# HGRN2's two pairs, SSD and LRU as lanes of their own, LRU in the buffers of the normed tokens, and four lanes for RWKV's scan

## The chip, the cores and the metric

The kernel runs on one core of a Trainium2 chip. The metric is the device time of one execution, in microseconds (us). TensorE (PE in the profile) does the matmuls and transposes, VectorE (DVE) and ScalarE (ACT) the elementwise work, GpSimd (POOL) a little of it, and SyncE (SP) issues the loads and stores.

## The reference

One inference step of a trunk with two layers on 384 tokens (128 of context, 256 latent) of width 1024, in float32. In each layer the normed and modulated tokens are projected to four head groups of width 256, each scanned forward and backward; their outputs are concatenated and projected back. Then follows an MLP of hidden width 4096.

```python
def trunk_layer(x, mod, lw, lb, shift_fn, states):
    h = rms_norm(x, lw['g_pre1']) * (1 + sc1) + sh1
    proj = h @ lw['w_in']
    p_rw, p_hg, p_ss, p_lr = jnp.split(proj, ...)
    y_rw, f_rw = rwkv7_mix(p_rw, lw, shift_fn, s_rw)   # 4 heads, state 64 x 64
    y_hg, f_hg = hgrn2_mix(p_hg, lw, lb, s_hg)         # 4 heads, gated linear attention
    y_ss, f_ss = ssd_mix(p_ss, lw, s_ss)               # short convolution, softplus dt, state 64 x 128
    y_lr, f_lr = rglru_mix(p_lr, lw, s_lr)             # short convolution, gates, a diagonal scan, gelu
    mix = jnp.concatenate([y_rw, y_hg, y_ss, y_lr], axis=-1) @ lw['w_out']
    x = x + g1 * rms_norm(mix, lw['g_post1'])
    h = rms_norm(x, lw['g_pre2']) * (1 + sc2) + sh2
    ff = jnp.square(jax.nn.relu(h @ lw['w1'])) @ lw['w2']
    return x + g2 * rms_norm(ff, lw['g_post2']), (f_rw, f_hg, f_ss, f_lr)
```

LRU, for one direction: `a = exp(log_a)`, `b = sqrt(1 - a*a) * (i * xc)`, the scan `h = a*h + b`, and at the end `(h_fw + h_bw) * gelu(y)`. The final context states of all four groups are outputs too.

## The kernel before

A layer is a mixer (`mixers`), then an MLP (`mlp`). The mixer projects the 384 tokens into 29 tiles of 128 columns. A tile is 24 matmuls of 384 columns, since weights and tokens are each split into a high and a low part of a faster matmul type (`split_tile`: ScalarE copies the high part, L612, VectorE subtracts the low one, L613). `ORDER` is the order of the tiles: 0, 1, 3, 5 for RWKV, then nine of HGRN2 (7 to 16), then 2, 4, 6, then the rest of HGRN2, SSD (17 to 24) and LRU (25 to 28). Finished tiles stand in seven `st` buffers; a tile is projected only when the one seven places before it has been taken.

The scans are generators, called lanes. Before, there are five: three threads `t0` to `t2` that share twelve groups of RWKV's scan, `rwkv` (inputs, vectors and outputs of RWKV), and `right`, which runs HGRN2's first pair of heads, its second pair, SSD and LRU one after the other. Their programs work in rounds. In a round every lane is visited once and goes on to its next `yield`; a lane that yields a condition (`need(n)`: tile n has been projected) is passed over until it holds. Then `supply` issues projections, four matmuls (PSTEP) at a step, until the round holds 3000 ns by the kernel's own reckoning of TensorE's work in `Tensor.put` (ROUND), and a step of the later modulations every 1 / MODS rounds. If `right` waits, the projections of the round are made up to URGENT // PSTEP = 6 steps, one tile. TensorE's instructions are tied to this order by dependencies (`T.ordered`); the other engines' instructions are ordered by the framework. All matmuls go through one helper line, L239, so the trace's rows are told apart by tiles.

When `right` has ended, `tail` becomes a lane: the output projection in eight units of 128 rows (order HGRN2, SSD, LRU, then RWKV's first and second half), each for three token tiles of six matmuls with 512 columns; it fills the rounds in which RWKV's last groups run. After its last unit come post-norm, residual and the norm ahead of the MLP (`residual`).

Results in PSUM stand in a ring of banks, r0, r1, r2 and two of h (and md in layer 1); a lane's step takes the next one. Projections have two banks of their own (pj).

HGRN2's pair takes five tiles, then six levels of products within chunks, its state and its output. Its tiles stand in a pool on the right side of SBUF that is opened and closed for each of HGRN2, SSD and LRU in turn. The modulation's weights have a pool of their own (`mw`, three buffers). `ahead` is a pool with two `wh` and two `wl` buffers for the first weights of the next stage. The normed tokens stand split in `hhi` and `hlo`. LRU does all its elementwise work after the gates in one step, L805 to L843.

## Time and profile before

| | |
|---|---|
| median of 3 runs | 1448.69 us (1448.4 to 1454.03) |
| the profiled execution | 1454.01 us, its span 1452.2 us |
| busy, share of the span | TensorE 90%, VectorE 63%, ScalarE 39%, GpSimd 4% |
| mean granted TensorE clock | 0.949 |

The profile is of one execution. Busy time of TensorE is taken from modelled ends of pipelined matmuls. "x<-y" is the tile that an instruction writes and those that it reads, "<-" behind an idle time what ended it. L239 and L242 are matmul and transpose for all callers. An fp32 matmul appears as two instructions.

### The profile page before, as it was taken

The numbers are of one execution on the slowest core, as the hardware profiler recorded it, in microseconds if no ns is written. First come the engines' busy times: TensorE is split into PE (matmuls) and PEld (weight loads), VectorE is DVE, ScalarE is ACT, GpSimd is POOL, SyncE is SP. The second block draws the span as 40 slices with busy tenths as digits, with TensorE's granted clock in tenths as the row PEclk, the third lists the DMA queues.
The fourth block names the chain that finished last, engine by engine and source line by source line (L and its number), as shares of the span: only waits on it lengthen the run. The fifth ranks groups of instructions, "written<-read, shape, count | busy, mean of one in ns | idle before, by whom it ended". The sixth has DMA issues, their size and how long they took to land.

```text
span 1452.2 us, 29173 instructions
## 1 busy us (share of the span) xinstructions
PE 1306.4 (90%) x12128; PEld 1128.8 (78%) x12128; DVE 918.6 (63%) x2149; ACT 570.0 (39%) x1016; POOL 51.1 (4%) x100
## 2 busy tenths in 40 slices
PE   7899987996878989999989999978878789999997
PEld 2678976886556888899869898867766589889986
DVE  4576576868557878386364866776767676434534
ACT  4452323441634333244254533342345434324422
POOL 0001020000001000000000111000000000000000
PEclk9799998999978999999999999989989889999999
DMA  9544421110047866463452112110103453433333
GB/s 333 173 165 147 154 75 53 60 53 31 19 174 276 309 219 220 153 233 128 155 182 84 59 60 76 43 57 31 52 16 119 162 177 132 154 128 129 131 130 117
DMA packets 56321, 187.59 MB, mean 129 GB/s; under 512 B 6492, under 2 KB 9580, under 8 KB 55164
## 3 DMA queue, kind: packets, MB, share of 16 engines
q1 hardware_dynamic: 56188, 185.73, 37.2%
q8 instruction: 95, 1.56, 0.4%
q14 instruction: 38, 0.31, 0.1%
HBM read 178.28 MB, written 7.43 MB: 128 GB/s over the span
## 4 chain that ended last, share of the span: by engine, by line
PE 71%; DVE 18%; DMA 5%; ACT 4%; issue 2%; SPq 0%; POOL 0%; DVEq 0%; ACTq 0%; POOLq 0%
PE pj L239 33%; PE r L239 18%; PE h L239 13%; PE md L239 6%; DMA w<-in_mod_w_dram 2%; DVE wl L613 2%; DVE ma L491 2%; DMA ms<-in_mod_w_dram 1%; DMA gp<-in_norm_g_dram 1%; ACT wh L612 1%; DVE rP L1385 1%; ACT junk L534 1%; DVE x L603 1%; PE r L242 1%; DVE sx L781 1%
## 5 line engine op out<-in xcount | busy, mean ns | idle before, releaser
L613 DVE TENSOR_TENSOR wl<-raw,wh 128x1024 fp32r<-128x1024 f32 x202 | 247.3, 1224 | 252.3 <-ACT wh L612 249.8
L239 PE MATMUL pj<-hhi,wl 128*128 128x384 f32 (+2 forms) x1024 | 347.0, 339 | 7.9 <-DVE wl L613 7.8
L612 ACT ACTIVATE wh<-raw 128x1024 fp32r<-128x1024 f32 x202 | 214.0, 1059 | 357.1 <-PE md L239 151.9
L239 PE MATMUL pj<-hlo,wh 128*128 128x384 f32 (+2 forms) x1024 | 347.4, 339 | 4.7 <-DVE hlo L566 4.2
L239 PE MATMUL pj<-hhi,wh 128*128 128x384 f32 (+2 forms) x1024 | 349.2, 341 | 1.5 <-ACT relu L625 1.4
L239 PEld LDWEIGHTS pj<-hhi,wh 128*128 128x128 f32 x1024 | 197.8, 193 | 16.0 <-issue 7.6
L239 PEld LDWEIGHTS pj<-hhi,wl 128*128 128x128 f32 x1024 | 197.7, 193 | 11.5 <-DVE wl L613 9.2
L239 PEld LDWEIGHTS pj<-hlo,wh 128*128 128x128 f32 x1024 | 198.0, 193 | 10.4 <-DVE hlo L566 4.6
L491 DVE SCALAR_TENSOR_TENSOR ma<-ms,csil,ma 128x1024 f32<-128x1024 f32 x70 | 87.1, 1277 | 3.5 <-DMA ms<-in_mod_w_dram 3.5
L1412 DVE TENSOR_TENSOR rI<-rI,r 128x256 f32<-128x256 f32 (+1 forms) x69 | 26.5, 392 | 23.2 <-PE r L239 22.5
L239 PE MATMUL r<-rI,rW 64*64 64x64 f32 x552 | 35.0, 225 | 2.1 <-ACT li L802 1.3
L626 DVE TENSOR_TENSOR relu<-relu 128x384 f32<-128x384 f32 x64 | 35.3, 551 | 2.4 <-ACT relu L625 2.3
L625 ACT ACTIVATE relu<-pj 128x384 f32<-128x384 f32 x64 | 30.3, 474 | 13.1 <-PE pj L239 13.1
L239 PEld LDWEIGHTS r<-rI,rW 64*64 64x64 f32 x552 | 26.7, 136 | 9.4 <-issue 3.7
L239 PE MATMUL pj<-w,csil 128*32 128x512 f32 x64 | 22.3, 756 | 11.9 <-DMA w<-in_mod_w_dram 11.9
L239 PE MATMUL r<-rI,rP 64*64 64x64 f32 x512 | 25.8, 233 | 6.0 <-DVE rI L1394 4.3
L239 PEld LDWEIGHTS r<-rI,rP 64*64 64x64 f32 x512 | 20.5, 144 | 12.3 <-issue 4.1
L239 PE MATMUL r<-rW,rI 64*64 64x64 f32 x448 | 28.7, 221 | 0.0
L1401 DVE TENSOR_TENSOR rW<-r,cst 128x128 f32<-128x128 f32 x64 | 17.5, 286 | 14.5 <-PE r L239 14.0
L1112 ACT ACTIVATE hk<-hK 128x384 f32<-128x384 f32 x24 | 13.5, 563 | 32.3 <-PE h L239 11.3
L578 POOL TENSOR_TENSOR xs<-x,scale 128x512 f32<-128x512 f32 x9 | 13.0, 1443 | 373.6 <-ACT junk L534 248.0
L239 PE MATMUL h<-wh,o 128*128 128x512 f32 x64 | 24.3, 459 | 2.0 <-ACT o L1589 2.0
(909 smaller groups left out, 2583.3 us busy)
## 6 DMA issues: line engine op xcount, KB each, us to landing
raw<-in_w_dram SPq DMA_DIRECT2D x128, 512.0 KB
raw<-in_win_dram SPq DMA_DIRECT2D x58, 512.0 KB
mw<-in_mod_w_dram SPq DMA_DIRECT2D x40, 512.0 KB
ms<-in_mod_w_dram SPq DMA_DIRECT2D x40, 512.0 KB
w<-in_mod_w_dram SPq DMA_DIRECT2D x16, 512.0 KB
raw<-in_wout_dram SPq DMA_DIRECT2D x16, 512.0 KB
xd<-x SPq DMA_DIRECT2D x9, 512.0 KB
x<-xd SPq DMA_DIRECT2D x9, 512.0 KB
```

What stands on the lines that cost most here:

```text
L239: return self.put(self.engine.matmul(out, left, right, **k), left, right)
L242: return self.put(self.engine.transpose(out, left, right), left, right)
L491: V.scalar_tensor_tensor(acc[:, r, :], w, c, acc[:, r, :], op0=OP.mult, op1=OP.add)
L534: self.S.activation(junk, v, AF.Square, scale=1.0 / 32, accum_out=acc[:, i:i + 1])
L603: self.V.scalar_tensor_tensor(v, ys[n], r, v, op0=OP.mult, op1=OP.add)
L612: self.S.activation(hi, v, AF.Copy)
L613: self.V.tensor_sub(lo, v, hi.bitcast(F32))
L625: self.S.activation(r, ps[:, :NT], AF.Relu)
L626: self.V.tensor_mul(r, r, r)
L781: self.V.scalar_tensor_tensor(out, x[:, j:j + GAP], w[j], out, op0=OP.mult, op1=OP.add)
L1401: V.tensor_mul(w, ps[:, :128].rearrange("p (u s) -> p u s", u=2), self.c(f"w{'fb'[d]}{h}")[:, None, :].to_broadcast([128, 2, 64]))
L1412: V.tensor_sub(flat[:, f], flat[:, f], ps[:, 128 if h == 32 else 0:256].rearrange("p (q s) -> p q s", s=64))
```

## The change

HGRN2's two pairs become lanes `hg0` and `hg1`, each with its own tiles (`hgrn(l, p)`); what both share moves to `hgrn_start` and `hgrn_end`. `right` waits until both have ended, norms HGRN2's output, and goes on to SSD. LRU becomes a lane that waits for all 29 projections and for the modulations to be done; its `r`, `a` and `t` stand in the buffers of `hhi` and `hlo`, the rest in `ahead`, and its elementwise work is cut into rounds of their own. RWKV's scan gets a fourth thread. The modulation's weights stand in `ahead`'s `wh` buffers. `tail` begins when all four side lanes have ended. A whole tile is now issued in a round in which no side lane ran. ORD is 10: all ten tiles of HGRN2 stand ahead of tiles 2, 4 and 6. The unchanged body of HGRN2 is left out below.

```diff
-NSTASH, HELD, MW = 7, 3, 3
+NSTASH, HELD = 7, 3
...
-ORD = 9
+ORD = 10
...
-    def modulation(self, l, v, W, hold, pool, bufs=MW):
+    def modulation(self, l, v, W, hold, pool, bufs):
...
-                w.append(pool.tile([128, 1024], F32, tag="mw", name=self.name("mw"), bufs=bufs))
+                tag, dt = ("mw", F32) if pool is not self.ahead else ("wh", F32R)
+                w.append(pool.tile([128, 1024], dt, tag=tag, name=self.name("mw"), bufs=bufs).bitcast(F32))
...
     def lru(self, l):
+
         V, S, T = self.V, self.S, self.T
-        lrw = self.mt([128, 1024], "lrw")
+        yield lambda: len(self.turns) == NTILE and self.moded
+        unit = lambda t: self.ahead.tile([128, 1024], F32R, tag=t, name=self.name("lu"), bufs=FRESH).bitcast(F32)
+        pair = lambda z: z.rearrange("p (q t) -> p q t", q=2)
+        lrw, rest = unit("wl"), unit("wl")
         self.nc.sync.dma_start(lrw, self.a["lrw"][l])
-        s0 = self.state("s_lr", [2, 2])
-        xc = self.mt([128, 2, GAP], "lxc")
+        W = 2 * GAP
+        xc, nst, s0 = pair(rest[:, 0:W]), pair(rest[:, W:W + 4]), pair(rest[:, W + 4:W + 8])
+        self.nc.sync.dma_start(s0, self.a["s_lr"][:, l])
+        r, a, t, i = [], [], [], []
+        for z in self.split_buffers():
+            z = z.rearrange("p k t -> p (k t)").bitcast(F32)
+            for n, v in enumerate((r, a, t)):
+                v.append(pair(z[:, n * W:n * W + W]))
+            i.append(pair(unit("wh")[:, 0:W]))
...
-        r, i, a = (self.mt([128, 4, GAP], k) for k in ("lr", "li", "la"))
-        for g, dst, bias in ((0, r, "ba"), (1, i, "bx")):
+        for d in range(2):
+            for g, dst, bias in ((0, r[d], "ba"), (1, i[d], "bx")):
+                for hf in range(2):
+                    q = 2 * d + hf
+                    ps = self.bank()
+                    T.matmul(ps[:, :GAP], lrw[:, (g * 4 + q) * 128:(g * 4 + q + 1) * 128], xc[:, hf, :],
+                             start=True, stop=True)
+                    S.activation(dst[:, hf, :], ps[:, :GAP], AF.Sigmoid, bias=self.p(bias, q))
+                yield 1
+        for fn, dst in ((AF.Tanh, t), (AF.Exp, a)):
             for q in range(4):
...
         for d in range(2):
-            V.tensor_mul(i[:, 2 * d:2 * d + 2, :], i[:, 2 * d:2 * d + 2, :], xc)
-        V.tensor_mul(t, t, i)
+            V.tensor_mul(i[d], i[d], xc)
+        yield 1
+        for d in range(2):
+            S.activation(r[d], a[d], AF.Square)
+            V.scalar_tensor_tensor(t[d], r[d], 1.0, t[d], op0=OP.add, op1=OP.mult)
+            V.tensor_scalar(t[d], t[d], -1.0, 0.0, op0=OP.mult, op1=OP.max)
+        for d in range(2):
+            S.activation(t[d], t[d], AF.Sqrt)
+        yield 1
         h = r
-        nst = self.mt([128, 2, 2], "lst")
         for q in range(4):
             d, hf = divmod(q, 2)
+            if hf == 0:
+                V.tensor_mul(t[d], t[d], i[d])
...
             e = 127 if d == 0 else 0
-            V.tensor_copy(nst[:, d, hf:hf + 1], h[:, q, e:e + 1])
+            V.tensor_copy(nst[:, d, hf:hf + 1], h[d][:, hf, e:e + 1])
+            yield 1
...
+        yield 1
...
+        self.outs["lru"] = out
...
-    def hgrn(self, l):
+    def hgrn_start(self, l):
+
+        self.hs0, self.hnst = self.state("s_hg", [2, 2, 64]), self.mt([128, 2, 2, 64], "hnst")
+        self.hout = self.mo.tile([128, 2, NT], F32, tag="o_hg", name=self.name("o_hg"))
+        self.hgs = {}
+
+    def hgrn(self, l, p):
+
         V, S, T, G = self.V, self.S, self.T, self.G
-        s0 = self.state("s_hg", [2, 2, 64])
-        nst = self.mt([128, 2, 2, 64], "hnst")
+        s0, nst = self.hs0, self.hnst
+        mt = lambda shape, tag: self.mt(shape, f"{tag}{p}")
...
+        room = self.ahead.tile([128, 1024], F32R, tag="wl", name=self.name("hr"), bufs=FRESH).bitcast(F32)
+        F, K, Q = (mt([128, W], n) for n in ("hF", "hK", "hQ"))
+        for d in range(2):
+            q, f, k = 2 * d + p, F[:, d * NT:d * NT + NT], K[:, d * NT:d * NT + NT]
+            ps = yield from self.need(T_HG + 5 * p + d)
...
+        sg = room[:, 0:NT]
+        S.activation(sg, ps[:, :NT], AF.Sigmoid)
+        V.scalar_tensor_tensor(sg, sg, self.p("hgn", p), ps[:, :NT], op0=OP.mult, op1=OP.mult)
+        self.hgs[p] = sg
+        yield 0
...
+        vc = room[:, NT:2 * NT].rearrange("p (c t) -> p c t", c=6)
...
+            nt = room[:, 2 * NT:2 * NT + n + 2] if h == 2 else mt([128, n + 2], f"ht{h}_")
...
+    def hgrn_end(self, l):
+        V = self.V
+        yield lambda: not {"hg0", "hg1"} & set(self.lanes)
+        os = [self.hout[:, p, :] for p in range(2)]
+        self.nc.sync.dma_start(self.o["n_hg"][:, l], self.hnst)
+        bc = yield from self.channel_rms(os, ("hq0", "hi0"))
...
+            V.tensor_mul(os[p], os[p], self.hgs[p])
+        return self.hout
...
         pool = lambda nm, side: self.tc.tile_pool(name=f"{nm}{l}", bufs=1, side=side, reuse_waits="tile")
 
         def right():
-            for nm in RIGHT:
-                with pool(nm, "right") as self.mp:
-                    self.outs[nm] = yield from getattr(self, nm)(l)
-        with pool("st", "left") as self.stash, pool("rwkv", "left") as rwkv, ExitStack() as aside:
-            mods = aside.enter_context(pool("mod", "right"))
-            flow = {"proj": self.projections(l, h), "mods": self.modulations(EARLY[l], mods)}
-            lanes = {"t0": self.rwkv_thread(0), "t1": self.rwkv_thread(1), "t2": self.rwkv_thread(2),
-                     "rwkv": self.rwkv(l), "right": right()}
+            self.outs["hgrn"] = yield from self.hgrn_end(l)
+            early.close()
+            with pool("ssd", "right") as self.mp:
+                self.outs["ssd"] = yield from self.ssd(l)
+        with pool("st", "left") as self.stash, pool("rwkv", "left") as rwkv, ExitStack() as early:
+            hgrn = self.mp = early.enter_context(pool("hgrn", "right"))
+            self.hgrn_start(l)
+            self.moded = False
+
+            flow = {"proj": self.projections(l, h), "mods": self.modulations(EARLY[l], self.ahead, FRESH)}
+            lanes = {"t0": self.rwkv_thread(0), "t1": self.rwkv_thread(1), "t2": self.rwkv_thread(2), "t3": self.rwkv_thread(3),
+                     "rwkv": self.rwkv(l),
+                     "hg0": self.hgrn(l, 0), "hg1": self.hgrn(l, 1), "right": right(), "lru": self.lru(l)}
+            self.lanes, side = lanes, {"hg0", "hg1", "right", "lru"}
             room, kind, waits = dict.fromkeys(lanes, rwkv), dict.fromkeys(lanes, 0), {}
+            room.update(dict.fromkeys(side, hgrn))
             self.T.ordered = True
 
             def visit(k):
...
                 n = 0
                 while self.T.ns < goal and n < most and next(flow[f], False):
                     n += 1
+                self.moded = self.moded or f == "mods" and n < most
                 return n
             supply("proj", self.T.ns + 1e9, FIRST * 24 // PSTEP)
             n, tail, made = 0, None, 0
...
                     for k in list(lanes):
                         if k not in seen and kind[k] <= turn and k != "tail" and visit(k):
                             seen.add(k)
-                if tail is None and "right" not in lanes:
-                    for f in flow.values():
-                        for _ in f:
-                            pass
-                    aside.close()
+                if tail is None and not side & set(lanes):
                     self.ring = ["r0", "r1"]
                     tail = self.tail(l)
                     lanes["tail"], kind["tail"], room["tail"] = tail, 2, None
                 if tail is None:
-                    made += supply("mods", begin + ROUND if n * MODS > made else 0, 1)
+                    if n * MODS > made and not self.moded:
+                        made += supply("mods", 1e18, 1)
                     got = supply("proj", begin + ROUND)
-                    if "right" in waits:
+                    if not side & seen:
                         got += supply("proj", begin + 1e9, URGENT // PSTEP - got)
                     assert seen or got, (l, n, list(lanes))
                 else:
```

## Rows read from the trace of the kernel before

**Rows 1.** The page: busy time by engine; one group: line, operation, count | busy, mean ns | idle.
```profile
PE 1306.4 (90%) x12128; PEld 1128.8 (78%) x12128; DVE 918.6 (63%) x2149; ACT 570.0 (39%) x1016; POOL 51.1 (4%) x100
...
L1412 DVE TENSOR_TENSOR rI<-rI,r 128x256 f32<-128x256 f32 (+1 forms) x69 | 26.5, 392 | 23.2 <-PE r L239 22.5
```

**Rows 2.** Four stretches: length; busy PE, PEld, DVE, ACT, POOL (counts); clock, DMA, GB/s.
```profile
69.10:376.20 307.10, 276.76 (x4042) 238.96 (x4041) 214.26 (x622) 120.46 (x237) 17.77 (x40) 0.96 0.27 90
376.20:460.60 84.40, 59.86 (x402) 44.87 (x401) 55.62 (x160) 41.55 (x79) 3.43 (x3) 0.84 0.45 164
787.50:1088.20 300.70, 266.10 (x3852) 238.98 (x3850) 208.79 (x613) 118.41 (x234) 18.54 (x40) 0.94 0.16 53
1088.20:1164.30 76.10, 61.70 (x466) 46.95 (x467) 53.11 (x156) 37.56 (x72) 3.07 (x3) 0.89 0.38 134
```

**Rows 3.** Waits of TensorE, 70 to 376 us: us in total, times, longest.
```profile
PE h L239 <- DVE dta L910: 8.7, 1, 8.7
PE h L242 <- DVE cry L302: 4.7, 1, 4.7
```

**Rows 4.** Waits of TensorE, 790 to 1088 us.
```profile
PE md L239 <- DVE dta L910: 8.1, 1, 8.1
PE r L242 <- DVE cry L302: 4.6, 1, 4.6
```

**Rows 5.** Timeline of VectorE, 940 to 962 us: start, us, instruction [idle before it].
```profile
942.61 0.18 DVE L903 TENSOR_TENSOR dtx<-r,par 128x24 f32<-128x24 f32 x1
942.73 0.62 DVE L781 SCALAR_TENSOR_TENSOR sx<-st,par,sx 128x386 f32<-128x386 f32 x1
...
952.60 0.16 DVE L910 TENSOR_TENSOR dta<-dtq,aneg 128x12 f32<-128x12 f32 x1
```

**Rows 6.** Waits of TensorE, 376.2 to 460.6 us.
```profile
PE r L239 <- DVE rkt L300: 12.0, 1, 12.0
```

**Rows 7.** Timeline of ScalarE and VectorE around LRU's elementwise work, layer 0.
```profile
375.12 1.28 ACT L811 ACT_TABLE_LOAD   x1
376.41 0.62 ACT L811 ACTIVATE la<-lr,spn 128x386 f32<-128x386 f32 x1
...
403.59 1.16 DVE L842 SCALAR_TENSOR_TENSOR o_lr<-o_lr,lr 128x128 f32<-128x128 f32 x4
```

**Rows 8.** Timeline of TensorE, layer 0, 372 to 461 us.
```profile
372.64 1.57 PE L239 MATMUL r<-lxc,lrw 128*128 128x386 f32 x4
...
376.24 0.33 PE L239 MATMUL r<-rvc,rT 64*64 64x64 f32 x4
...
439.33 0.63 PE L239 MATMUL h<-wl,o 128*128 128x512 f32 x2
439.80 0.62 PE L239 MATMUL h<-wh,o 128*128 128x512 f32 x2
...
444.92 0.48 PE L239 MATMUL pj<-pick,sh 128*128 128x512 f32 x1
...
460.57 0.51 PE L239 MATMUL pj<-hhi,wh 128*128 128x256 f32 x2
```

**Rows 9.** Timeline of TensorE, layer 1, after a wait of 4.58 us.
```profile
1111.88 1.05 PE L239 MATMUL h<-wl,o 128*128 128x512 f32 x2
1112.74 1.05 PE L239 MATMUL h<-wh,o 128*128 128x512 f32 x2
```

**Rows 10.** Timeline, 385 to 387 us: two steps of an RWKV thread.
```profile
385.88 0.45 PE L239 MATMUL r<-rw,rI 64*64 64x64 f32 x8
...
386.53 0.45 PE L239 MATMUL r<-rI,rW 64*64 64x64 f32 x8 [0.21 <-ACT ru L1435]
```

**Rows 11.** Timeline of VectorE, 395 to 445 us: first and last of an RWKV output's norm.
```profile
425.82 0.28 DVE L1305 TENSOR_REDUCE rsm<-ryt 128x2 f32<-128x128 f32 x1
...
430.86 0.29 DVE L1311 TENSOR_TENSOR ryt<-ryt,rky 128x128 f32<-128x128 f32 x1
```

**Rows 12.** Instructions on the tile `mw`, 60 to 260 us: idle before them, us, times.
```profile
  issue: 1.3, 4
```

More of the change, by code (lines that the diff above doesn't have):

```diff
@@ new lines, in hgrn @@
+        ps = yield from self.need(T_HG + 5 * p + 2)
+        qc = mt([128, NT], "hq")
+        S.activation(qc, ps[:, :NT], AF.Sigmoid)
+        V.tensor_mul(qc, qc, ps[:, :NT])
+        for d in range(2):
+            V.tensor_mul(Q[:, (1 - d) * NT:(2 - d) * NT], qc, F[:, d * NT:d * NT + NT])
+        ps = yield from self.need(T_HG + 5 * p + 3)
+        vi = mt([128, NT], "hi")
+        S.activation(vi, ps[:, :NT], AF.Copy)
+        ps = yield from self.need(T_HG + 5 * p + 4)
+        sg = room[:, 0:NT]
@@ new lines, in hgrn @@
+        att = mt([128, 6, 64], "hatt")
+        yield 0
+        ps = self.bank()
+        for c in range(6):
+            self.heads(ps[:, c * 64:c * 64 + 64], vi[:, c * 64:c * 64 + 64], qc[:, c * 64:c * 64 + 64])
+        V.tensor_mul(att, ps[:, :NT].rearrange("p (c t) -> p c t", c=6),
+                     stack[:, None, :].to_broadcast([128, 6, 64]))
+        tot = F
+        for h in LEVELS:
+            n = NT // h
+            k = mt([128, NT], "hk")
+            S.activation(k.rearrange("p (b i t) -> p b i t", i=2, t=h), sides(K, h), AF.Copy)
@@ new lines, in hgrn @@
+        yield 0
+        po = self.bank()
+        for c in range(6):
+            o = po[:, c * 64:c * 64 + 64]
+            more = [(prev[d, c], Q[:, (1 - d) * NT + c * 64:(1 - d) * NT + c * 64 + 64])
+                    for d in range(2) if (d, c) in prev]
+            self.heads(o, vc[:, c, :], att[:, c, :], True, not more)
+            for j, (state, q) in enumerate(more):
+                self.heads(o, state, q, False, j == len(more) - 1)
+        S.activation(self.hout[:, p, :], po[:, :NT], AF.Copy)
@@ L1486, in projections, with modulations @@
                 yield True
[L1488 removed]
+    def modulations(self, parts, pool, bufs):
         for k, v, W in parts:
```

183 lines of the change are left out of this document (56 added, 127 removed).

## Prediction

> **What bounds the kernel now.** I read the page's busy lines first. TensorE is busy 90% of the span, VectorE 63% [rows 1]; so TensorE's idle time and the time it spends at the lower clock are what can be won. Next I cut the two mixers into a front (start to round 74, or 71) and an end (from there to the MLP's first matmul) [rows 2]. Layer 0: a front of 307.1 us with 276.8 busy, so 30.3 idle, and an end of 84.4 with 59.9 busy, 24.5 idle. Layer 1: 300.7 with 34.6 idle, and 76.1 with 14.4. The reader is to see that all four hold some 104 us of idle TensorE, and that the change touches nothing else. The waits then name the idle time: in each front one wait of 8 us ends with the SSD softplus (`dta`) and one of 4.7 with the RMS of SSD (`cry`) [rows 3, 4]; in layer 0's end one of 12.0 ends with a small VectorE instruction of RWKV's output, `rkt` [rows 6].
>
> How the rounds are placed in the trace: I counted the yields of each lane and the nanoseconds that `Tensor.put` adds, by the rules of `supply`. That is the kernel's own reckoning, it orders TensorE's work, and I take rounds from it, no time. Before, both layers have 84 rounds. Last projected tile: round 58 or 59 (both layers). LRU ends, and `tail` begins, in round 74 (layer 0) and 71 (layer 1); RWKV ends in round 84. Round 74 begins at 376.24 [rows 8].
>
> **What the change does to the rounds.** The same matmuls are issued, in another order. Three rules matter. (1) The tile supply. Before, whenever `right` waits, a whole tile (URGENT//PSTEP = 6 steps) is issued in that round. After, only if no side lane ran; a lane that takes one tile and waits for the next has run. So while HGRN waits for its tiles they come in every other round, and the four RWKV threads take more of each 3000 ns. By my count the first pair starts its flips in round 11 (layer 1: 10) instead of 7, the second in 26 (24) instead of 25 (23): the pairs hardly overlap. (2) RWKV's tiles 2, 4, 6 now come behind ten HGRN tiles, so its second input pair is ready in round 40 (35) instead of 32; the fourth thread still brings RWKV's end to round 83 (78) from 84. (3) LRU waits for all 29 tiles, and the last comes in round 68 (66): LRU's gates lie beside SSD's last rounds, and its elementwise rounds, 75 to 82 (73 to 80), are the last of all. `tail` begins when LRU ends, in round 82 (80), not 74 (71). So rounds 75 to 81 have no projection and no output matmul to fill them. That is the price; what is bought is that TensorE has projections until round 68, and that LRU's VectorE and ScalarE work no longer stands in RWKV's way in one block.
>
> **The end of the mixer, layer 0.** At the start of round 74 both kernels have issued the same matmuls to within 1 us of the reckoning. Then, after the change: round 74 itself, a pair of gates at 1.6 us [rows 8], RMS and a thread, 3.3. Rounds 75 to 82: RWKV's last thread has six single steps, at 0.65 for one from matmul to matmul through ScalarE [rows 10] and about 1 with LRU's instructions between, 6.0; two RWKV outputs, each 5.3 from `rsm` to the end of its scaled `ryt` [rows 11], 10.6; the RMS wait of 4.7 less the gate pair that now covers it, 3.0; together 19.6. Then the output projection, 8 x 18 matmuls; two take 0.47 [rows 8], so 33.8. After a long gap they start at the low clock: two took 0.86 after a wait in layer 1 [rows 9]; some 11 of them cost 2.1. Norms, from the last output matmul to the MLP, as before: 444.92 to 460.57, 15.7. Sum 74.5 for 84.4: -9.9. It rests on LRU not holding the tail up. LRU's elementwise work took 29.6 us, from 375.12 to 404.75, among other work [rows 7]; TensorE needs it for the fifth of the units, at 19.6 + 16.9 = 36.5 after round 75. Covered.
>
> **Layer 1.** Both kernels have issued the same at round 71. After: rounds 71 and 72 with two gate pairs and a thread's last step, 6.1; the RMS wait's rest 1.8; rounds 73 to 78 with four single steps, one output chain and the end of another, 4 + 5.3 + 3 = 12.3; then 33.8 + 2.1 + 15.7. Sum 71.8 for 76.1: -4.3. LRU is due at 12.3 + 16.9 = 29.2, against 29.6: no slack here.
>
> At this place a rule of the Trainium skill (ScalarE: Activation LUTs, What ACT_TABLE_LOAD costs) speaks against the change: a switch of function set is a load of about 1283 ns and a drain of about 1380 more. The row shows a load of 1.28 us [rows 7], and the next activation starts 0.01 after its end; no drain stands out. By the page, as an estimate, four switches of LRU would bring layer 1's LRU 5.5 us later and the time to 1433; the trace has them within the 29.6, so I give this no chance beside rival (a).
>
> **The fronts.** The RMS waits of SSD, 4.7 and 4.6, leave the fronts, as they are counted in the ends above: -9.3. The softplus: its chain takes from 942.61 to 952.60, 10.0 us [rows 5], and between its instructions of 0.17 stand 14 of the short convolution at about half a microsecond, whose tiles had been projected ahead. After the change `right` itself waits for those tiles (17 on come from round 39 on), so they can't stand there; the chain of 22 dependent steps, at 0.2 each, and some of RWKV's vectors make 6 of the 10. -4 in each layer, -8. The convolutions go to rounds that projections fill; without that cover the 8 come back.
>
> Against this stand more lanes per round. A TensorE step that takes a PSUM bank waits for the eviction of its last user. Four lanes share five banks in layer 0 (six in layer 1); now five or six lanes do. No trace here shows that. My count has 75 rounds with five lanes or more, in both layers together, for 22 before. Below, nothing; above, two evictions by RWKV's inverse, 0.39 each [rows 1], in each of the 53 more: 41. I take about a quarter, 11, as a lane's own wait mostly ends later than that for its bank.
>
> At nothing: the modulation weights in two buffers shared with `wh` for three of their own. TensorE sat idle before their matmuls for 1.3 us in all, on no DMA [rows 12]; a step comes every 2.5 rounds of over 3 us, which covers a load; if not, the next raw tile on SP's queue is late as well. LRU's weights are loaded in round 69 for use in round 71, before beside SSD; the raw queue is empty by then. LRU's tiles in the split tokens wait for the last projection, which it waits for anyway.
>
> **Sum.** -9.9 - 4.3 - 9.3 - 8 + 11 = -20.5. The profiled execution took 1454.01 (span 1452.2, 1.8 around it), as long as the longest of the runs shown, whose median is 1448.69. So some 1433.5 beside the profiled one, and 1448.7 - 20.5 = 1428 for the median.
>
> **Rivals.** (a) LRU holds the tail. If its VectorE and ScalarE instructions come first in the queues and RWKV's output chains behind them, the starved stretch is 29.6 in place of 19.6 and 12.3 in both layers, +27: 1455, slower by 0.4%, and by more if RMS waits too. It decides from about 24 us per layer on. For it: in the trace LRU's scans ran in one block while RWKV's reduction waited. Against it: the block is cut into seven rounds now. (b) The banks bind in the crowded rounds. 41 in place of 11: 1458. The Trainium skill (Perfetto Trace Analysis, Optimization Strategy) says that the same gap repeating on the engine that should be saturated can mean too little PSUM for the next tile. The trace's waits in the fronts are single ones [rows 3, 4], with four lanes. (c) The gain is larger: the lanes fill most of the fronts' remaining idle time (65 less the 17 counted; say 20 of it) and no bank wait shows: 1428 - 20 - 11 = 1397, half of it 1412. (d) The lanes do nothing: the pairs run one after the other and the fronts stay as they are but for the RMS; the softplus wait stays, the ends count, half the bank price too, and 4 for LRU late in layer 1: 1448.7 - 14.2 - 9.3 + 5.5 + 4 = 1435.
>
> **Chances.** Forecast (1414 to 1441) 0.47, (c) below it 0.13, (d) 0.12, (a) 0.15, (b) 0.13. A measurement of this kernel tells about 0.5%, 7 us, from no change. Faster: the forecast, (c) and half of (d), 0.66, less 0.01 for its upper edge: 0.65. Slower: two thirds of (a), whose end is at 0.4%, and half of (b), 0.16. Same: the rest, 0.19. Range 1402 to 1456; the forecast's own is 1414 to 1441.
>
> **What would show it.** Right: the softplus wait is 4 to 5 us; the waits on `cry` have shrunk; before the output projection TensorE has a stretch of 12 to 20 us with a few small matmuls, with VectorE on LRU and RWKV; from its end to the MLP some 51 us with hardly a gap. The second HGRN pair's levels come after the first's. Wrong: that stretch is near 30 us; or repeated gaps of 0.3 to 0.5 in the fronts before RWKV's steps; or LRU's split `o` is waited for in the tail.

## Result and the profile after

The changed kernel takes 1467.59 us (median of 4 runs, 1463.46 to 1469.24), the kernel before 1450.04 beside it: a ratio of 1.0109, 95% interval 1.0089 to 1.013. It is 1.1% slower, where 1428 and a gain were forecast. The profiled execution has a span of 1466.5 us, 14.3 more than before's.

TensorE is busy 89% of the span, for 90% in [rows 1].

The four stretches of [rows 2] in after. Layer 0's cut is again the start of round 74, at 379.2, layer 1's that of round 71, at 1093.3; layer 1 starts 1.6 us later than before, and so does its window.

```profile
69.10:379.20 310.10, 280.74 (x4112) 243.23 (x4111) 214.48 (x634) 121.40 (x238) 18.14 (x41) 0.94 0.28 91
379.20:462.90 83.70, 57.31 (x322) 44.56 (x321) 54.36 (x152) 40.66 (x81) 2.77 (x2) 0.82 0.48 164
789.10:1093.30 304.20, 274.07 (x4020) 245.83 (x4019) 214.09 (x638) 118.64 (x235) 18.12 (x41) 0.94 0.17 55
1093.30:1179.40 86.10, 58.45 (x302) 43.98 (x301) 54.27 (x144) 47.87 (x86) 2.77 (x2) 0.78 0.33 116
```

The fronts grew by 3.0 and 3.5 us, layer 0's end fell by 0.7, layer 1's grew by 10.0; the rest of the span fell by 1.5. The reader is to see the counts: in front of the cut TensorE has now done 70 and 168 matmuls more than before, behind it 80 and 164 fewer, and layer 1's end is longer all the same, with 27.7 us idle for 14.4.

TensorE's waits in after, a fence for each stretch: layer 0's front and end, then layer 1's front and end.

```profile
PE h L239 <- DVE dta L921: 5.2, 1, 5.2
PE r L239 <- DVE ryt L1333: 4.9, 2, 3.6
PE r L239 <- DVE rS L1473: 3.0, 2, 2.0
```

```profile
PE r L239 <- DVE ryt L1333: 8.0, 1, 8.0
PE h L239 <- DVE ryt L1333: 5.5, 1, 5.5
PE pj L239 <- ACT wh L613: 2.0, 1, 2.0
...
PE h L242 <- DVE cry L302: 0.8, 1, 0.8
```

```profile
PE r L239 <- DVE dta L921: 6.2, 1, 6.2
PE r L239 <- DVE ryt L1333: 3.9, 1, 3.9
PE h L239 <- DVE ryt L1333: 3.7, 1, 3.7
```

```profile
PE h L239 <- DVE ryt L1333: 12.1, 1, 12.1
...
PE r L239 <- DVE ryt L1333: 3.6, 1, 3.6
```

The softplus (`dta`) is waited for 5.2 and 6.2 us instead of 8.7 and 8.1 [rows 3, 4]; the RMS of SSD (`cry`) left the fronts and is waited for 0.8 us in layer 0's end and not at all in layer 1's. What grew is `ryt`, RWKV's normed output: 4.9 and 7.6 us in the fronts, 13.5 and 15.7 in the ends.

Before, TensorE waited for the same norm 1.6 and 4.0 us in the fronts, 15.8 in layer 0's end and 1.9 in layer 1's. The 12.0 of [rows 6] is part of the 15.8: the matmul that waited reads `ryt`, and on VectorE its norm stood around LRU's block, 14.8 us long (TensorE's row, then the norm's first and last instruction on VectorE, before):

```profile
406.29 0.69 PE L239 MATMUL r<-cst,ryt 64*64 64x64 f32 x8 [11.96 <-DVE rkt L300]
```
```profile
391.34 0.28 DVE L1305 TENSOR_REDUCE rsm<-ryt 128x2 f32<-128x128 f32 x1
...
405.85 0.29 DVE L1311 TENSOR_TENSOR ryt<-ryt,rky 128x128 f32<-128x128 f32 x1
```

In all, the waits for RWKV's norm went from 23.3 us to 41.7. TensorE's idle time in the mixers grew by 10.1, so its other waits became shorter. In layer 0's end the wait for the norm is old, in layer 1's end it is new. What makes the wait of 12.1 is seen on VectorE (after; start, us, instruction):

```profile
1112.89 0.28 DVE L1327 TENSOR_REDUCE rsm<-ryt 128x2 f32<-128x128 f32 x1
...
1117.78 0.16 DVE L295 TENSOR_SCALAR rkm<-rvr 128x2 f32<-128x2 f32 x1
...
1117.98 0.42 DVE L837 TENSOR_TENSOR_SCAN hlo<-hlo 128x128 f32<-128x128 f32 x1
1118.32 0.13 DVE L300 TENSOR_TENSOR rkt<-rky 128x2 f32<-128x2 f32 x1
1118.37 0.74 DVE L837 TENSOR_TENSOR_SCAN hlo<-hlo,lu 128x256 f32<-128x256 f32 x1
1119.03 0.13 DVE L301 TENSOR_TENSOR rkt<-rkt,rkm 128x2 f32<-128x2 f32 x1
...
1120.84 0.95 DVE L849 TENSOR_TENSOR hhi<-hhi,hlo 128x772 f32<-128x772 f32 x1
1121.71 0.15 DVE L302 SCALAR_TENSOR_TENSOR rky<-rkt,rky 128x2 f32<-128x2 f32 x1
1121.78 0.95 DVE L845 TENSOR_TENSOR lu<-lu,o_lr 128x768 f32<-128x768 f32 x1
...
1123.23 0.29 DVE L1333 TENSOR_TENSOR ryt<-ryt,rky 128x128 f32<-128x128 f32 x1
```

`rkt`, `rky` and `ryt` are the steps of RWKV's norm, each dependent on the one before; the scans and the wide products between them are LRU's. From `rsm` to the end of `ryt` the chain takes 10.6 us; the two in layer 0's end take 6.9 and 7.0, the other one in layer 1's end 4.4. VectorE takes its instructions one after the other, so each short step of one lane waits for a long one of the other. The Trainium skill (PSUM — Partial Sum Buffer, Engine vs sequencer instructions) says that VectorE's queue is strictly first in, first out; the rows agree.

What stands behind that wait, on TensorE, layer 1 (idle before an instruction in brackets):

```profile
1101.36 2.94 PE L239 MATMUL h<-lu,lu 128*128 128x386 f32 x4
...
1123.58 0.69 PE L239 MATMUL h<-cst,ryt 64*64 64x64 f32 x8 [12.06 <-DVE ryt L1333]
1124.20 0.79 PE L239 MATMUL md<-lora,rlw 32*128 32x128 f32 x2
1124.92 1.22 PE L239 MATMUL pj<-wh,o 128*128 128x512 f32 x2
1125.94 1.05 PE L239 MATMUL pj<-wl,o 128*128 128x512 f32 x2
...
1132.45 0.63 PE L239 MATMUL pj<-wl,o 128*128 128x512 f32 x2
```

The output projection begins 1.3 us behind the wait, at the low clock (two matmuls in 1.05 us, 0.63 once it is over). What its first four units read, HGRN's and SSD's outputs, was ready when the last of `o_ss` was written, at 1097; they stood behind the wait because `tail` begins when LRU has ended.

### The profile page after: what moved, and what is told of

The parts are those of the page before. It is cut to its first block, busy times and chain, and to the rows that moved or that the text cites. A ratio compares the mean times of both kernels' runs of the same rounds, so it can differ in the third digit from the quotient of the medians.

```text
span 1466.5 us, 29196 instructions
## 1 busy us (share of the span) xinstructions
PE 1310.9 (89%) x12128; PEld 1134.5 (77%) x12128; DVE 920.4 (63%) x2155; ACT 578.8 (39%) x1028; POOL 49.9 (3%) x100
## 4 chain that ended last, share of the span: by engine, by line
PE 66%; DVE 19%; DMA 7%; ACT 5%; issue 2%; SPq 0%; POOL 0%; DVEq 0%; ACTq 0%
PE pj L239 31%; PE r L239 17%; PE h L239 12%; PE md L239 5%; DVE wl L614 3%; DMA w<-in_mod_w_dram 2%; DVE ma L492 2%; ACT wh L613 2%; DMA ms<-in_mod_w_dram 2%; DMA gp<-in_norm_g_dram 1%; DMA raw<-in_wout_dram 1%; ACT junk L535 1%; DVE sx L782 1%; DVE rP L1407 1%; DVE x L604 1%
## 5 line engine op out<-in xcount | busy, mean ns | idle before, releaser
L626 ACT ACTIVATE relu<-pj 128x384 f32<-128x384 f32 x64 | 30.3, 474 | 13.2 <-PE pj L239 13.2
L239 PE MATMUL r<-rI,rW 64*64 64x64 f32 x528 | 31.9, 222 | 0.0
L1129 ACT ACTIVATE hk<-hK 128x384 f32<-128x384 f32 x24 | 13.5, 564 | 42.3 <-PE r L239 28.4
L239 PE MATMUL pj<-wh,o 128*128 128x512 f32 x64 | 22.8, 441 | 3.5 <-ACT wh L613 3.5
L1434 DVE TENSOR_TENSOR rI<-rI,h 128x256 f32<-128x256 f32 (+1 forms) x45 | 17.0, 383 | 12.5 <-PE h L239 11.9
```

The costliest lines, as they stand in the source:

```text
L239: return self.put(self.engine.matmul(out, left, right, **k), left, right)
L626: self.S.activation(r, ps[:, :NT], AF.Relu)
L1129: S.activation(k.rearrange("p (b i t) -> p b i t", i=2, t=h), sides(K, h), AF.Copy)
L1434: V.tensor_sub(flat[:, f], flat[:, f], ps[:, 128 if h == 32 else 0:256].rearrange("p (q s) -> p q s", s=64))
```

## Experiments

Eighteen kernels. The table has the ratio to the kernel before with its interval, and of the profiled execution both mixers together, from each layer's first projection matmul to the MLP's first: length, TensorE's idle and busy time in it, and the mean granted clock by layer. The matmuls are the same in all but the last two.

```
                               ratio  (interval)        length  idle   busy   clock
before                         1                        812.6  108.1  704.5  0.93 0.93
after                          1.0109 (1.0089-1.0130)   829.4  118.2  711.2  0.91 0.91
e1_tail_early                  1.0032 (1.0010-1.0054)   820.2  107.3  712.9  0.91 0.92
e2_lru_light                   1.0007 (0.9986-1.0028)   810.5  105.8  704.7  0.92 0.93
e7_last_unit_first             1.0063 (1.0044-1.0081)   822.7  118.2  704.6  0.91 0.92
e4_bank_less                   1.0144 (1.0107-1.0180)   835.4  121.9  713.5  0.90 0.91
e6_old_tiles                   0.9983 (0.9965-1.0001)   805.7  110.7  695.0  0.91 0.93
e16_tiles_and_tail             0.9957 (0.9937-0.9976)   796.0  102.8  693.2  0.93 0.92
b1_before_new_tiles            1.0177 (1.0156-1.0198)   839.8  122.0  717.8  0.90 0.93
e8_three_threads               1.0098 (1.0063-1.0133)   825.5  109.9  715.6  0.92 0.93
e5_lru_behind_ssd              1.0140 (1.0101-1.0179)   835.5  115.1  720.4  0.89 0.91
e56_lru_behind_ssd_old_tiles   0.9914 (0.9881-0.9948)   794.6  106.5  688.1  0.93 0.93
e56_three_threads              1.0114 (1.0094-1.0134)   828.8  106.4  722.5  0.91 0.90
e567_last_unit_first           0.9942 (0.9922-0.9962)   795.2  109.0  686.2  0.93 0.93
b4_fourth_thread               0.9971 (0.9953-0.9990)   816.0  101.4  714.6  0.89 0.91
a_round_3400                   1.0144 (1.0124-1.0163)   835.9  121.8  714.1  0.89 0.91
e56_round_3400                 1.0055 (1.0039-1.0071)   814.1  117.5  696.5  0.91 0.93
e56_round_2600                 0.9985 (0.9972-0.9998)   809.0  111.7  697.3  0.91 0.93
f_after_filler                 1.0181 (1.0145-1.0216)   836.7  104.0  732.7  0.91 0.93
f_b4_filler                    1.0032 (1.0015-1.0048)   823.5   95.2  728.4  0.93 0.92
```

Length, idle, busy and clock are of one execution each, and the ratio is of all. The kernel before itself took 1446.35 to 1461.24 us in the 17 executions beside one of these kernels, at mean granted clocks of 0.956 to 0.942, so some us of busy time between two rows can be the execution. The profiled execution of `e8_three_threads` lies 7.5 us below its median, that of `b4_fourth_thread` 7.1 above. What lies outside the mixers took 632 to 645 us, so a ratio doesn't follow from a length.

Length, idle and busy come from windows over the two mixers, as these of before and of after:

```profile
43.31:460.57 417.26, 358.17 (x4539) 304.77 (x4538) 285.52 (x825) 175.96 (x341) 21.20 (x43) 0.93 0.32 110
769.00:1164.32 395.32, 346.32 (x4458) 304.40 (x4456) 268.15 (x782) 163.72 (x316) 21.61 (x43) 0.93 0.19 66
```

```profile
42.38:462.91 420.53, 360.17 (x4538) 308.42 (x4537) 284.85 (x828) 177.35 (x345) 20.92 (x44) 0.91 0.34 110
770.57:1179.43 408.86, 351.05 (x4460) 308.31 (x4458) 274.65 (x795) 174.29 (x332) 20.90 (x43) 0.91 0.20 65
```

So of the 16.8 us that the mixers grew, 10.1 are idle time and 6.7 are the same matmuls at a lower clock. In the us below, a ratio is multiplied by 1451; the expectations are compared with the medians.

### The ends

The output projection early:

```diff
-                if tail is None and not side & set(lanes):
+                if tail is None and "right" not in lanes and self.gated:
...
             if k == 0:
                 yield from self.need("p0")
+            if GROUPS[k // 2] == "lru":
+                yield from self.need("lru")
```

> Kernel after, but the output projection begins as soon as HGRN and SSD are out and LRU's gates are issued; it waits for LRU before LRU's two units. Theory A (the loss sits in the mixers' ends: no output matmul is issued until LRU's last round, while RWKV's norm chain waits between LRU's instructions on VectorE): the waits for ryt of 5.5 and 8.0 us in layer 0 and of 12.1 in layer 1 are filled with the 72 matmuls of the first four units; some 10 us less in layer 0 and 15 in layer 1, about 1442. Rival B (the tiles: the HGRN pairs starve, so that all lanes end late, and LRU's work stands on RWKV's last steps wherever the output matmuls are): the waits move behind the four units and at most 10 us are won, 1458. Rival C (too few PSUM banks for the crowded rounds): it says nothing of the ends; those fall as in A.

11 us less than after (median 1457): B's number, 1458, and not A's 1442. The early matmuls took 9 us out of layer 1's mixer, where the two waits for `ryt` fell from 15.7 to 10.2 us. Layer 0's mixer stayed at 420.5, with waits of 9.3 and 5.6. The first is RWKV's norm again: the row names a copy of LRU's states, which ended beside it, but the matmul reads `ryt`.

```profile
402.36 0.69 PE L239 MATMUL r<-cst,ryt 64*64 64x64 f32 x8 [9.33 <-DVE lu L840]
```

From `rsm` at 390.64 to `ryt` at 402.21 this norm takes 11.6 us, for 6.9 in after, since the splits for the output units now stand in it beside LRU's pieces. To fill the stretch is worth something; the waits themselves stay. When `tail` begins, the lanes' ring is cut to two banks, so the edit also takes banks from the lanes some rounds earlier; what that costs isn't separated.

LRU without its elementwise work behind the gates, on VectorE and on ScalarE, all rounds kept:

```diff
-            S.activation(r[d], a[d], AF.Square)
-            V.scalar_tensor_tensor(t[d], r[d], 1.0, t[d], op0=OP.add, op1=OP.mult)
-            V.tensor_scalar(t[d], t[d], -1.0, 0.0, op0=OP.mult, op1=OP.max)
...
-                V.tensor_tensor_scan(v(h), v(a), v(t), init, op0=OP.mult, op1=OP.add)
...
-        S.activation(y2, y2, AF.Tanh, scale=GELU_C)
```

> Kernel after, with LRU's elementwise work left out behind its gates: no products, squares, scans or tanh of the output gate (the two LRU units of the output are not the reference's); its matmuls, rounds and the place of the output projection stay. Theory A: RWKV's norm chains take 5 us again, the waits for ryt in the ends fall from 5.5, 8.0 and 12.1 to about 4 each, and the stretch before the output projection goes from 25 and 21 us to some 19 and 13: about 1450. If the chains alone or the low clock made the stretch (rival to A): 1464 or more. Rival B: 1460, as the rounds stay. Rival C: 1465, as the banks stay.

15 us less than after (1452): A's number. The same norm chain of layer 1, alone on VectorE:

```profile
1100.18 0.29 DVE L1311 TENSOR_REDUCE rsm<-ryt 128x2 f32<-128x128 f32 x1
...
1102.10 0.16 DVE L300 TENSOR_TENSOR rkt<-rky 128x2 f32<-128x2 f32 x1
1102.30 0.16 DVE L301 TENSOR_TENSOR rkt<-rkt,rkm 128x2 f32<-128x2 f32 x1
...
1103.86 0.29 DVE L1317 TENSOR_TENSOR ryt<-ryt,rky 128x128 f32<-128x128 f32 x1
```

4.0 us for 10.6, and its wait 4.4 for 12.1; in layer 0's end the waits are 3.3 and 4.5 for 5.5 and 8.0. That LRU's instructions between the steps make the long waits of the ends is shown. That all of the 15 us are the change's isn't: the kernel before had 15.8 us of such waits in layer 0's end, and LRU's work was not taken out of it.

The last unit of the output weights ahead of the MLP's first two, in after and in the best kernel below:

```diff
-        self.prepare(a["w1"][l, n] for n in range(FRESH))
...
         w = self.unit(a["wout"][l, 1])
+        self.prepare(a["w1"][l, n] for n in range(FRESH))
```

> Kernel after, with the last unit of the output weights loaded and split ahead of the MLP's first two. In after the last unit's matmuls waited 2.0 and 1.4 us for the split on ScalarE, and 2.2 us of low clock came behind it in layer 0. If the split is late because two other units stand before it on ScalarE and VectorE: 4 to 5 us less, 1463. If the units' loads bound it, or the MLP's first matmuls then wait for theirs: 1467.

> The pairs as lanes, four threads, LRU behind SSD and the old rule of the tile supply, and the last unit of the output weights is loaded and split ahead of the MLP's first two. The last output matmuls wait for RWKV here, not for their weights: within 3 us of 1441. If the weights' split on ScalarE holds the end: 1436.

7 us in after, more than the 4 to 5 expected; nothing in the other (0.9942 for 0.9914, the intervals overlap), where RWKV and not the split is late. But in after the two mixers' idle time did not move (118.2 both): what fell is busy time. In layer 0 the output projection takes 35.7 us from its first matmul to its 144th, for 39.3 in after, and the norms behind it are 1.9 longer; in all, layer 0's mixer is 1.0 shorter. Layer 1's is 5.7 shorter, and 4.4 of these lie ahead of its last tile, where both kernels issue the same. Why the clock was higher there is open.

### The tiles

The old rule in after; with the early output projection; the new rule alone in before:

```diff
-                    if not side & seen:
+                    if {"hg0", "hg1", "right"} & set(waits):
```
```diff
-                    if "right" in waits:
+                    if "right" not in seen:
```

> Kernel after, with the rule of before for the tile supply: a whole tile in each round in which an HGRN pair or the lane behind them waits for one. By the count of its rounds the pairs end in rounds 18 and 23 in place of 22 and 37, SSD in 56 in place of 75 and 71, LRU in 69 and 60 in place of 82 and 80, RWKV in 75 in place of 83 and 78. Rival B: the output projection now has RWKV's last rounds beside it, both ends fall by 10 to 15 us and the fronts by a few, 1440 or below. Theory A alone: the ends fall as they do with the early output projection, but the fronts lose their projections by about as much: 1445 to 1460. Rival C: more lanes at once in rounds 8 to 23, more bank waits, 1465 or more.

> Both edits together: the old rule of the tile supply and the early output projection. Rounds as with the old rule alone (RWKV ends in round 75, LRU in 69 and 60, SSD in 56); the output projection may begin once LRU's gates are out, some 6 rounds before LRU's end in layer 0. Theory A: layer 0 of the old rule alone still has 32 us of idle TensorE behind its last tile; some 10 of them are filled: 1438, about 1% below before. Theory B alone: the tiles were the whole of it, and nothing more is won: 1447.

> Kernel before with only the new rule of the tile supply. One lane asks for tiles here, HGRN, SSD and LRU one after the other. By the count of rounds the last tile comes in round 60 and 58 (58 and 58 before), LRU ends in 79 and 73 (74 and 71), RWKV in 84 as before. Theory B as it now stands (the rule costs where two pairs and SSD ask for tiles in turn): a few us, 1452 to 1458. Rival F (the rule alone makes the whole loss): 1465 or more.

The old rule gives 18 us back (median 1450, in A's range), together with the early output projection 22 (median 1447, B's number); the 4 between them are at the edge of the intervals. The new rule alone costs the kernel before 26, more than the whole change. I had taken it for a matter of the pairs (B, "a few us"); that was wrong, F's number came. By the table its cost is 13.9 us of idle and 13.3 of busy time, although by the count LRU ends only five and two rounds later. One place where idle time comes from is seen in layer 0, around 280 us, on VectorE of that kernel:

```profile
273.61 0.54 DVE L1305 TENSOR_REDUCE rsm<-ryt 128x6 f32<-128x384 f32 x1
...
284.00 0.61 DVE L781 SCALAR_TENSOR_TENSOR sx<-st,par,sx 128x386 f32<-128x386 f32 x1
284.53 0.15 DVE L301 TENSOR_TENSOR rkt<-rkt,rkm 128x6 f32<-128x6 f32 x1
284.61 0.41 DVE L1412 TENSOR_TENSOR rI<-rI,h 128x256 f32<-128x256 f32 x1
284.94 0.15 DVE L302 SCALAR_TENSOR_TENSOR rky<-rkt,rky 128x6 f32<-128x6 f32 x1
...
288.40 0.55 DVE L1311 TENSOR_TENSOR ryt<-ryt,rky 128x384 f32<-128x384 f32 x1
```

Its first RWKV norm stands among SSD's convolutions (`sx`) and a thread's inverse and takes 15.3 us; TensorE waits 6.2 for it in one go. But the same norm is nearly as long in the kernel before, 13.2 us, without the convolutions, and TensorE waits 1.6 there:

```profile
275.90 0.55 DVE L1305 TENSOR_REDUCE rsm<-ryt 128x6 f32<-128x384 f32 x1
...
288.56 0.55 DVE L1311 TENSOR_TENSOR ryt<-ryt,rky 128x384 f32<-128x384 f32 x1
```

So this place gives 4.6 of the 13.9 us. All waits for RWKV's norm together are 28.1 us for 23.3. Most of what the rule costs this kernel isn't traced to a place.

One PSUM bank less:

```diff
-        self.ring = ["r0", "r1", "r2", "h", "h"] + ([] if EARLY[l] else ["md"])
+        self.ring = ["r0", "r1", "h", "h"] + ([] if EARLY[l] else ["md"])
```

> Kernel after, with one PSUM bank less in the ring that the lanes share (four in layer 0, five in layer 1, in place of five and six). Rival C (banks bind in the crowded rounds): each of the 75 rounds with five lanes or more pays another eviction of 0.4 us or so, 1490 or more, and waits of that size stand in the fronts. Theories A and B: under 5 us more, at most 1473.

0.35% or 5 us more than after, with intervals that overlap, at the edge of A and B, far from C; the fronts' waits are mostly single long ones, and waits for `rI` sum to 1.8 us in layer 0's front of after and to 4.7 in layer 1's. C falls, and with it the rule cited in the prediction (the Trainium skill, Perfetto Trace Analysis, Optimization Strategy) as the reading for this case: too little PSUM isn't it.

### The parts

Three threads in after; LRU as before, behind SSD, with four threads, under the new rule and under the old; the latter with three threads; the fourth thread alone in before, with the modulation's weights in the `wh` buffers as in after. The lines of the first and of the second edit, the second without LRU's body, which is that of before:

```diff
-            lanes = {..., "t2": self.rwkv_thread(2), "t3": self.rwkv_thread(3),
+            lanes = {..., "t2": self.rwkv_thread(2),
```
```diff
+            with pool("lru", "right") as self.mp:
+                self.outs["lru"] = yield from self.lru(l)
```

> Kernel after with three RWKV threads in place of four. By the count of rounds the last tile comes in round 63 and 60, LRU ends in 77 and 74, RWKV in 84: seven to ten of RWKV's rounds stand beside the output projection, none did with four. Theory A: the ends gain 5 to 8 us each, the fronts, with fewer steps per round beside the same tiles, lose as much or less: 1455 to 1465. Rival D (the fourth thread brings a gain that the ends hide): 1475 or more.

> Kernel after, but with the LRU of before, in a pool of its own behind SSD, uncut between its gates and its end; it ends in round 81 and 77, RWKV in 83 and 78. Theory A: it isn't the cutting of LRU that costs, but that LRU stands last and the output projection behind it: 1462 to 1472, and a wait of RWKV's norm for a block of LRU. Rival E (the cuts let LRU's instructions in between the steps of RWKV's norm; in one block they cost nothing more than before): 1455 or below.

> The same with the old rule of the tile supply: the pairs end in rounds 18 and 23, SSD and LRU by round 62, RWKV in 75, so 13 of RWKV's rounds stand beside the output projection in both layers. Theories A and B: 1440 to 1448. Rival E: within 3 us of the old rule with LRU as a lane, 1450.

> The pairs as lanes, LRU behind SSD and the old rule of the tile supply, with three RWKV threads: the right lane ends in round 62 as with four, RWKV in 84 instead of 75, so nine of its rounds stand beyond the output matmuls. If the fourth thread is what shortens the end (theory A with the count): 1452 to 1462 against 1441 with four. Rival G (the fourth thread does nothing, as the run with three threads under the new rule gave 1468 for 1468): 1438 to 1445.

> Kernel before with the fourth RWKV thread alone (and the modulation weights in the weights' buffers, as in after, for the room). By the count of rounds RWKV ends in 75 and LRU in 77 and 74 (84, 74 and 71 before): no round of RWKV is left beside the output projection. Balance: RWKV's norms wait among LRU's instructions and the output matmuls come behind, as in after: 1455 to 1470. The thread is worth its 27 us by itself: 1425 to 1432.

Under the new rule the fourth thread is worth nothing that can be told (1.0098 and 1.0109): D falls, and A's 1465 is within the interval. Under the old rule, with the pairs as lanes, it is worth 29 us (1.0114 to 0.9914), more than A had; alone, 4 us, between the two numbers given.

LRU's cuts aren't the fault (E falls: 1.014). But A's wait for a block of LRU didn't come either. With LRU behind SSD, under the new rule, the waits for RWKV's norm in the ends are short, 15.2 us for 29.2 in after, and the kernel is no faster: TensorE now waits 4.6 in one go for LRU's split `o`, 4.9 for the RMS of SSD and 4.2 for a weight's split, and its busy time is 9.2 us longer. Short norms alone don't make a fast kernel. `e56_lru_behind_ssd_old_tiles`, the fastest, waits 30.3 us for them, the kernel before 23.3.

Put together in one order: the fourth thread 0.9971; with the pairs as lanes 0.9914; with LRU as a lane 0.9983; with the new rule 1.0109. So the pairs and the thread together gain 12 us, LRU's lane costs 10, the rule 18. In other orders the shares differ: the rule costs 26 in the kernel before and 33 with LRU behind SSD (0.9914 to 1.014), and under the new rule LRU's lane costs nothing. Pairs as lanes with three threads cost 17 (1.0114): HGRN, SSD and LRU are then through by round 62, and 22 rounds of RWKV are left. The kernel with four threads, LRU behind SSD and the old rule, 0.9914, beats both given kernels.

### What stayed open: the length of a round, and the clock

```diff
-ROUND, URGENT, MODS, PSTEP, FIRST = 3000, 24, 0.4, 4, 4
+ROUND, URGENT, MODS, PSTEP, FIRST = 3400, 24, 0.4, 4, 4
```

> Kernel after with 3400 ns of matmuls to a round in place of 3000, so that tiles come faster. By the count the last tile comes in round 61 and 60 (68 and 66), SSD ends in 69 and 65 (75 and 71), LRU in 75 and 74 (82 and 80), RWKV in 78 and 75 (83 and 80). Balance: three rounds of RWKV stand beside the output projection in layer 0 and one in layer 1, 8 to 15 us less than after: 1453 to 1460. Meeting: anywhere within 12 us of 1467.

> The pairs as lanes, four threads, LRU behind SSD and the old rule (1441), with 3400 ns to a round: the last tile comes in round 45 and 42 (55 and 46), everything else stays in its round. Balance: the rounds from 45 to 62, with SSD and LRU, have no projections beside them, 3 to 8 us more: 1444 to 1449. Meeting: anywhere within 12 us of 1441.

> The same with 2600 ns to a round: the last tile comes in round 58 and 57, so that SSD has projections beside it in layer 1 as well, and everything else stays in its round. Balance: 3 to 8 us less than 1441: 1433 to 1438. Meeting: anywhere within 12 us of 1441.

Balance fails: after with longer rounds has LRU and RWKV out earlier and is 5 us slower, not 8 to 15 faster; the best kernel is 20 us slower with longer rounds, far more than 3 to 8, and 10 slower with shorter ones. Meeting has two of the three; the 20 lie outside its 12 as well. So the count of rounds doesn't give the time, and what does is not settled by these.

The fourth thread alone saves 6.7 us of idle time and loses 10.1 of busy time, in an execution 7.1 us above its median. Its clock is lower in all of them: 0.933 to 0.947 in its twelve, 0.948 to 0.957 in the 23 of before beside it. Matmuls without a use in the rounds between the last tile and the output projection:

```diff
+                    if len(self.turns) == NTILE and n > 50:
+                        ps = self.bank("pj")
+                        for _ in range(4):
+                            self.T.matmul(ps[:, :128], self.c("ident"), self.c("ident"), start=True, stop=True)
```

> Kernel after, with four matmuls without a use (128x128 by 128 columns, into a projection's bank) behind each round between the last projected tile and the output projection: 14 rounds or so in each layer, some 0.9 us a round by the 0.22 to 0.28 us that such matmuls take. If the clock of these rounds (0.82 and 0.79 as means of the ends, 0.61 in the worst stretch) comes from TensorE having too little to do there: it rises to 0.9 or more, the matmuls that count take 4 to 8 us less, and as the waits cover most of the fillers the time falls by 3 to 6 us to 1461 to 1465. If the clock doesn't follow: the fillers stand behind the waits, 5 to 15 us more, 1472 to 1482.

> The same fillers in the kernel before with the fourth thread (1446): 15 rounds in layer 0 and 10 in layer 1, where the granted clock was 0.61 with TensorE busy 37 of 54 us. If the clock follows: 0.85 or more there, 5 to 10 us less of busy time on the matmuls that count, the time 1438 to 1444. If not: 1452 to 1462.

10 and 9 us more: in time as if the clock had not followed. It did follow (in the second case mean clocks of 0.946 to 0.957 in the executions with fillers, 0.933 to 0.947 without). This stretch of layer 0, from the last tile to RWKV's end, in the kernel before with the fourth thread, without and with the fillers:

```profile
341.50:395.50 54.00, 36.86 (x292) 29.19 (x292) 35.95 (x146) 17.29 (x38) 0.00 (x0) 0.61 0.18 61
```

```profile
341.50:397.90 56.40, 42.52 (x390) 36.77 (x388) 36.09 (x146) 19.71 (x42) 0.00 (x0) 0.82 0.21 72
```

The granted clock rose from 0.61 to 0.82, and the stretch is 2.4 us longer: 98 more matmuls cost more than the clock gave. With their 38.6 and 32.8 us taken off, the mixers' busy time is 17 and 19 us lower than without fillers (they overlap other matmuls, so this is an upper bound). The low clock is a price of the rounds without projections, but it isn't won back so.

## Why the prediction was wrong

**The rounds** came as counted, from the program: in layer 0 the last tile in round 68, LRU's end in 82, RWKV's in 83; in layer 1 66, 80 and 78.

**"At the start of round 74 both kernels have issued the same matmuls"** failed: 70 and 168 more by then in after, 4.0 and 8.0 us of busy time. The fronts, forecast at -9.3 - 8 + 11 for both layers, came out at +6.5: 12.0 of moved work less 5.4 of idle time.

**The fronts' gains** were of the right kind and went to another wait. The RMS left (0.8 and nothing for 4.7 and 4.6), the softplus gave 3.5 and 1.9 of the 4 each (three convolutions and RWKV's vectors still stand in its chain). But idle time fell only from 30.3 to 29.4 and from 34.6 to 30.1, as `ryt` and RWKV's states came in. That the later projections buy something was the belief behind it: "what is bought is that TensorE has projections until round 68". TensorE's order is fixed, a wait stands ahead of the projections of its round, and they don't fill it. The old rule in after (-18 us) and the new one in before (+26) show that this purchase is a loss; by which waits, the runs show in part only.

**The bank price**, 11, seems too high: a whole bank less costs 5.

**The ends** are where the forecast lost most, 9.2 and 14.3 us. Round 74 was 3.2 (3.3 forecast). The starved stretch of layer 0, from 382.4 to the first output matmul at 407.8, is 25.4 for 19.6; in layer 1 rounds 71 and 72 take 10.9 for 7.9, the rest to 1124.9 20.7 for 12.3. The step that failed is "two RWKV outputs, each 5.3": that row [rows 11] has no LRU beside it, and the chains took 6.9, 7.0 and 10.6. The price with LRU beside it stood in the trace of before, 14.8 us from 391.34 to 406.14, behind the wait of 12.0 that the prediction names [rows 6]; in layer 0's end TensorE waits 13.5 us for the norm where it had waited 15.8, and 15.7 for 1.9 in layer 1's. I asked whether LRU holds up the output projection (it did not: no wait for its split `o`) and not whether it holds up RWKV's norm. Rival (a) named that mechanism, at 29.6 a layer, and I gave it 0.15 on the ground that the block is cut into rounds. The cuts are on paper; in VectorE's queue the pieces stand one by one between the norm's steps. The run without LRU's elementwise work shows it.

**The output projection**: 40.1 and 39.4 us for 33.8 + 2.1. In layer 0 the last unit waits 2.0 for its split behind the MLP's first two and starts again at the low clock; in layer 1 the first unit takes 7.1 (1124.92 to 1131.99) for the second's 4.2. The clock was sized by its first 11 pairs in one place; in layer 0 it came twice. **The norms**: 15.0 and 15.1 for 15.7, right.

**At nothing**: right. No wait of TensorE in after's fronts and ends goes by a load. The drain behind a table switch (the Trainium skill, ScalarE: Activation LUTs, What ACT_TABLE_LOAD costs) was not seen either; ScalarE in layer 1's end:

```profile
1097.59 1.28 ACT L815 ACT_TABLE_LOAD   x1
1098.88 0.58 ACT L815 ACTIVATE hlo<-md,par 128x386 f32<-128x386 f32 x1
...
1103.87 1.28 ACT L815 ACT_TABLE_LOAD   x1
1105.16 1.05 ACT L815 ACTIVATE lu<-h,par 128x386 f32<-128x386 f32 x2
```

A load of 1.28, and the next activation 0.01 behind it. But LRU's gates and its exponentials now alternate, as one direction is through before the other's gates are: seven loads between 1095 and 1117 where the prediction had four for LRU.

What isn't settled: why an order that differs by a few rounds gets a busy time from 686 to 722 us for the same matmuls, beyond that the low clock goes with rounds of small matmuls and waits; and a rule that gives the time from the rounds. That lanes' instructions meet on VectorE and make TensorE wait is shown for the ends of after and for layer 0's end of before; that it makes the cost of the new rule and the scatter of the round lengths is only argued.

## What to carry to other kernels

A count of rounds tells what is issued when, not what it costs: before moving a lane, list for each chain of dependent small instructions which long ones of other lanes will share its engine's queue, and price the chain by that sum (4.0 us alone, 10.6 among LRU's). Take the price from the place of the old trace that has the same company, not from the cleanest one. Work that can fill an in-order engine has to be issued ahead of the wait it is to cover; here that was the output projection, and holding it back for the last lane left the stretch empty (issued earlier, it gained 9 us in layer 1 and nothing in layer 0). Try the parts of a change apart: two of the four here gained 0.9% together, and the other two, in that order, cost over twice that.

## What the runs showed of the hardware that I had not expected

TensorE's clock moves a kernel with 90% busy TensorE as much as its waits do. The same matmuls of the two mixers took from 686.2 us (mean granted clock 0.93) to 722.5 (0.91 and 0.90). The kernel with 722.5, `e56_three_threads`, has less idle time than before (106.4 us for 108.1) and is 1.1% slower; its five executions had mean clocks of 0.936 to 0.940, the eleven of before beside them 0.949 to 0.953. The lowest clock stands where small matmuls, LRU's gates and waits are left and no projections: 0.61 in a stretch that was 68% busy (36.86 of 54.00 us, the kernel before with the fourth thread), 0.50 (1.2 of the 2.4 GHz) in layer 0's end of after, where TensorE had worked 4.71 of 14.20 us:

```profile
393.50:407.70 14.20, 4.71 (x58) 3.69 (x55) 13.11 (x45) 6.15 (x11) 0.00 (x0) 0.50 0.24 75
```
